# A third PSUM buffer for two kinds of products, and an earlier place for the tiles of one of them

## The chip, the core and the metric

The kernel runs on one core of a Trainium2 chip. The core has five engines that work side by side, each through its own list of instructions in order: TensorE (PE) for matrix products, VectorE (DVE), ScalarE (ACT), GpSimd (POOL) and SyncE (SP). Here POOL only issues indirect transfers and SP only plain ones. Products land in PSUM, which has eight banks of 128 partitions x 512 float32; everything else lies in SBUF. The metric is the device time of one execution in microseconds, the median of several runs.

## What is computed

One layer on 1024 frames of 1024 channels: a projection, two recurrent groups, an output projection, and then PEER, a retrieval over 16384 single-neuron experts. The change lies in PEER:

```python
q = (xb @ wq).reshape(TOK_BLOCK, PEER_HEADS, PEER_QDIM)
s1 = jnp.einsum('thd,kd->thk', q[..., :PEER_HALF], k1)
s2 = jnp.einsum('thd,kd->thk', q[..., PEER_HALF:], k2)
v1, i1 = lax.top_k(s1, PEER_TOPK); v2, i2 = lax.top_k(s2, PEER_TOPK)
...
sc, cidx = lax.top_k(cand, PEER_TOPK)
e = i1[cidx // PEER_TOPK] * PEER_NKEYS + i2[cidx % PEER_TOPK]
g = jax.nn.softmax(sc, axis=-1)
act = jax.nn.gelu(jnp.einsum('thkd,td->thk', u_tab[e], xb))
return jnp.einsum('thk,thkd->td', g * act, v_tab[e])
```

So each token picks 16 experts for each of 8 heads, weighs them by a softmax, and sums their output rows, each times the gelu of its input row with the token.

## The kernel before

The 1024 tokens are eight blocks of 128. Three blocks (NG) are **gathered**: the chosen rows of both tables are fetched, one token's expert to a partition, and worked on DVE, one row of 128x1024 at a time (`row`, summed into `hb`). Five blocks (ND = 5, TD = 640 tokens) are **dense**: for all 16384 experts, in 128 tiles of 128 experts, the kernel forms gelu(u x) and multiplies it with a weight that is zero where an expert was not chosen. Both run at once, since the first loads DVE and the transfers, and the second PE.

The program goes through these stages:

- **Up to 370 us**: projection, recurrent groups, output projection (`wop`). Then the norm's transposes (`x2t` of `xn`, split into `xDh` and `xDl`).
- **The query**: `qp`, PE products with weights `wqr` that SP loads and ACT and DVE split into `wqh` and `wql`, three products each for float32 accuracy. The result `qt` goes with `kT` into scores (`sp`, `sc`). The first head's query (`q_2940`, from weights `woh` and `wol` that lie in the output projection's pool) is made just ahead by `query0`. Scores of the dense blocks go to DRAM (`S_d`). DVE takes the top 16 of the gathered blocks meanwhile.
- **Build and ahead**: for each dense block, `topk` on DVE (`s` from `S_d`, `v`, `ix`, `scv`, `ci`, the softmax `ex` on ACT, `oh`, `if`), a PE transpose `gt` into `kt`, and then the dense weight matrix from one-hot products: for four tokens at a time DVE and ACT make `ohA` and `ohB` (DVE one of the four `ohB`, ACT the other three with six instructions), PE multiplies them (`gp`), ACT copies `gp` to `gs`, and SP stores `gs` to `G_d`, 2 MB at a time. Beside it `ahead` computes the first products of 97 of the 128 expert tiles: SP loads `ur`, ACT and DVE split it (`uh`, `ul`), PE makes two halves of 320 tokens in 24 matmuls each (`ap`, in `first`), ACT applies gelu (`aa`), and SP stores `aa` to `A_d`. `aa` lies in the pool `ph1`, three tiles of 128x640 float32.
- **Dense** (from 1512 us): the other 31 first products, and the second products `vp` and `total`, in an order written out by hand.

Three things set the order around the change. A planner (`Merge`) with estimated costs interleaves the threads as the code is recorded. The recording layer then orders the instructions of each engine again by its own estimate of when buffers come free, so another number of buffers moves instructions; only the dense stage is exempt. And a pool that is opened where another was closed makes its first users wait for the last users of the old one.

In PSUM, `ppa` has two banks (queries and first products), `ppt` two for `pt` and two for `pb` (the one-hot products), and two banks of the eight are used by no pool until the dense stage. In SBUF `ph1` is opened behind the query's pools `pq` and `pkg`, where these lay.

Of the kernel before, what the change touches and what calls it, by code (L numbers as in the profile page):

```python
# [7 lines left out]
F32 = mybir.dt.float32  # L8
# [7 lines left out]
PSUM = bass.MemoryType.PSUM  # L16
DRAM = bass.MemoryType.DRAM

P = 128
# [949 lines left out]
HALF = TD // 2  # L969
# [9 lines left out]
def peer(tc, a, cst, pools, h, nx, mg):  # L979
# [19 lines left out]
    ppa = pools.open("ppa", bufs=2, space=PSUM)  # L999
    ppt = pools.open("ppt", bufs=2, space=PSUM)  # L1000
    pa = lambda n: ppa.tile([P, 512], F32, tag="a", name=n)
    pt = lambda n: ppt.tile([P, 512], F32, tag="t", name=n)
    pb = lambda n: ppt.tile([P, 512], F32, tag="b", name=n)

    def split_to(hi, lo, src):
        S.activation(hi, src, AF.Copy)
# [319 lines left out]
    def load_split(pool, src, shape, tag):  # L1326
# [5 lines left out]
        split_to(h, lo, r)  # L1332
        return h, lo

    def first(dst, u):
        uh, ul = u
        for i in range(2):
            sl = slice(HALF * i, HALF * i + HALF)
            p_ = pa("ap")[:, :HALF]
            for k in range(8):  # L1340
                PE.matmul(p_, uh[:, k], xDl[:, k, sl], start=(k == 0), stop=False)
                PE.matmul(p_, ul[:, k], xDh[:, k, sl], start=False, stop=False)
                PE.matmul(p_, uh[:, k], xDh[:, k, sl], start=False, stop=(k == 7))
            yield
            S.activation(dst[:, sl], p_, AF.Gelu_apprx_tanh)
            yield
# [61 lines left out]
    def ahead():  # L1408
        fetch_u()
        yield  # L1410
        while made[0] < NA:
            kept = made[0] == NA - 1
            t = ph1.tile([P, TD], F32, name="aa", tag="hr", bufs=3)
            if kept:
                tile(0, 2).hr = t
            j = order[made[0]]
            for n, _ in enumerate(first(t, nextu[0])):
                if n == 0:
                    fetch_u(NA + 1)
                yield  # L1420
            if not kept:
                nc.sync.dma_start(A_d[j], t)
                mg.dma(320)
            made[0] += 1
            nextu.pop(0)
        mg.flag("ahead")
# [17 lines left out]
    mg.run([(1.0, topks()), gr], until="q")  # L1444
    mg.run([], until="chosen")
    pools.close("pkg", "pq")
    ph1 = pools.open("ph1")
    pk2 = pools.open("pk2", bufs=2)

    def build():  # L1450
# [13 lines left out]
        nc.sync.dma_start(gts[c], G_d[c])  # L1464

    mg.run([], until="g")
    pools.close("pk2", "ppt")


    ppr = pools.open("ppr", bufs=1, space=PSUM)  # L1470
# [18 lines left out]
    def second(p_, b, t, first, last, halves=(0, 1)):  # L1489
        bs = slice(b * P, b * P + P)  # L1490
        for i in halves:
            ns = slice(512 * i, 512 * i + 512)
            PE.matmul(p_[:, i], t.hh[:, bs], t.vl[:, ns], start=first, stop=False)
            PE.matmul(p_[:, i], t.hl[:, bs], t.vh[:, ns], start=False, stop=False)
            PE.matmul(p_[:, i], t.hh[:, bs], t.vh[:, ns], start=False, stop=last)
# [236 lines left out]
def body(tc, a):  # L1732
    nc = tc.nc
    pools = Pools(tc)
    pcst = pools.open("cst")
    ident = pcst.tile([P, P], F32, name="ident")
    make_identity(nc, ident)
    iota = pcst.tile([P, P], F32, name="iota")
    nc.gpsimd.iota(iota, pattern=[[1, P]], base=0, channel_multiplier=0, allow_small_or_imprecise_dtypes=True)
    mg = Merge(nc)  # L1740
    cst = dict(ident=ident, iota=iota)
    fpools, h, nx = front(tc, a, cst, ND, mg)
    peer(tc, a, cst, fpools, h, nx, mg)
    pools.close("cst")
# [65 lines left out]
```

## Time and profile before

| what | us |
|---|---|
| median of 3 runs | 2625.98 |
| lowest and highest run | 2618.97, 2636.02 |
| the profiled execution | 2620.74 |
| its span, first to last instruction | 2619.0 |

Over the whole span PE is busy 96%, PE's weight loads 87%, DVE 90%, ACT 50% and POOL 43% of the time, and the granted clock of PE is 0.985 on average. Busy shares are means over stages, and a busy PE is not PE at its peak. A row of instructions reads: start, duration, engine, line, operation, output<-inputs, and in brackets the idle time of the engine just before, with what ended it. A row of the waits reads: who waited for whom, the sum in us, how many times, the longest. A row of the chain reads: start, duration, what. The line is L146 nearly everywhere, since one helper records all instructions; so names of tiles tell the work apart.

### The profile page before, as it was taken

The page shows a single profiled execution, that of the slowest core. Times are in us where ns is not written, and L with a number is a line of the kernel's source. Part 1 is how long each engine was busy: PE and PEld are TensorE (multiplying, and loading weights), DVE is VectorE, ACT ScalarE, POOL GpSimd, SP SyncE. Part 2 cuts the span into 40 slices and gives each one's busy share as a digit, 9 for nine tenths or more (in the row PEclk, how much of TensorE's full clock was granted, in tenths as well). Part 3 has the DMA queues.
Part 4 walks back from the last instruction along what each step waited for, and adds up shares of the span by engine and source line. Part 5 has one row for each costly group of instructions (what it writes and reads, how often), then busy time and mean ns, then how long its engine had stood idle before and what let it go on. Part 6 is the DMA issues. An engine that isn't in the chain of part 4 may idle for free.

```text
span 2619.0 us, 40771 instructions
## 1 busy us (share of the span) xinstructions
PE 2503.9 (96%) x14623; PEld 2268.0 (87%) x14623; DVE 2365.3 (90%) x4556; ACT 1321.8 (50%) x2402; POOL 1130.8 (43%) x777
## 2 busy tenths in 40 slices
PE   7998999998999999999999999999999999999997
PEld 6776889998999999999999888888888888888885
DVE  7898659998999999999999399999989999999997
ACT  6566434332683965938739643333444433333442
POOL 0000000343664756848547054555445555554551
PEclk9999999999999999999999999999999999999999
DMA  5113124587899998999989899999989999999993
GB/s 183 30 43 108 61 91 137 189 287 285 305 394 310 360 388 307 397 344 349 399 297 377 277 336 343 346 343 342 342 321 346 344 342 341 343 347 341 340 339 132
DMA packets 302539, 753.31 MB, mean 288 GB/s; under 512 B 28928, under 2 KB 127424, under 8 KB 297600
## 3 DMA queue, kind: packets, MB, share of 16 engines
q0 software_dynamic: 110592, 402.70, 42.2%
q1 hardware_dynamic: 186048, 337.85, 36.4%
q10 hardware_dynamic: 5696, 10.15, 1.2%
q8 instruction: 115, 1.88, 0.3%
q14 instruction: 88, 0.72, 0.1%
HBM read 663.44 MB, written 85.98 MB: 286 GB/s over the span
## 4 chain that ended last, share of the span: by engine, by line
PE 62%; DVE 22%; DMA 7%; ACT 4%; issue 3%; ACTq 0%; SPq 0%; DVEq 0%
PE vp L146 26%; PE ap L146 17%; PE total L146 7%; PE qp L146 4%; DMA A_d<-aa 3%; PE gp L146 3%; PE wop L146 3%; DVE row L146 2%; DVE oh L146 2%; DVE ul L146 2%; DVE hb L146 2%; ACT ohB L146 1%; DVE ix L146 1%; DVE ci L146 1%; DVE v L146 1%
## 5 line engine op out<-in xcount | busy, mean ns | idle before, releaser
L1264 POOL DMA_INDIRECT row<-in_peer_u_dram,idx x384 | 564.8, 1471 | 958.5 <-DVE scv L146 471.0
L1264 POOL DMA_INDIRECT row<-in_peer_v_dram,idx x384 | 563.2, 1467 | 440.6 <-DVE hb L146 302.4
L146 PE MATMUL ap<-xDl,uh 128*128 128x320 f32 x2048 | 650.9, 318 | 14.3 <-ACT aa L146 12.0
L146 PE MATMUL ap<-xDh,ul 128*128 128x320 f32 x2048 | 642.8, 314 | 8.8 <-DVE ul L146 8.8
L146 PE MATMUL ap<-xDh,uh 128*128 128x320 f32 x2048 | 641.5, 313 | 0.0
L146 DVE SCALAR_TENSOR_TENSOR hb<-row,act,hb 128x1024 f32<-128x1024 f32 x384 | 491.5, 1280 | 4.6
L146 DVE CUSTOM_DVE_ANT_0 row<-row,xg 128x1024 f32<-128x1024 f32 x384 | 457.6, 1218 | 7.1 <-DMA row<-in_peer_u_dram,idx 6.6
L146 PE MATMUL vp<-vl,hh 128*128 128x512 f32 x1024 | 400.2, 391 | 9.4 <-DVE h L146 6.7
L146 PEld LDWEIGHTS ap<-xDl,uh 128*128 128x128 f32 x2048 | 390.4, 191 | 17.7 <-ACT aa L146 13.7
L146 PEld LDWEIGHTS ap<-xDh,ul 128*128 128x128 f32 x2048 | 390.5, 191 | 11.9 <-DVE ul L146 10.5
L146 PE MATMUL vp<-vh,hl 128*128 128x512 f32 x1024 | 400.2, 391 | 0.0
L146 PE MATMUL vp<-vh,hh 128*128 128x512 f32 x1024 | 399.0, 390 | 0.0
L146 PEld LDWEIGHTS ap<-xDh,uh 128*128 128x128 f32 x2048 | 389.8, 190 | 0.0
L146 ACT ACTIVATE gq<-gt 128x640 f32<-128x640 f32 x128 | 174.9, 1366 | 306.5 <-DVE hr L146 302.8
L146 PEld LDWEIGHTS vp<-vl,hh 128*128 128x128 f32 x1024 | 192.6, 188 | 50.4 <-DVE h L146 7.6
L146 PEld LDWEIGHTS vp<-vh,hh 128*128 128x128 f32 x1024 | 192.8, 188 | 40.9
L146 PEld LDWEIGHTS vp<-vh,hl 128*128 128x128 f32 x1024 | 192.5, 188 | 38.8
L146 ACT ACTIVATE ohB<-ohB,kt 128x128 f32<-128x128 f32 x480 | 205.3, 496 | 0.0
L146 ACT ACTIVATE aa<-ap 128x320 f32<-128x320 f32 x194 | 84.4, 436 | 237.2 <-PE ap L146 206.0
L146 PE MATMUL gp<-ohB,ohA 128*128 128x128 f32 x1280 | 183.7, 278 | 17.9 <-ACT gs L146 8.9
L146 DVE TENSOR_TENSOR h<-h,vp 128x1024 f32<-128x1024 f32 x128 | 155.7, 1217 | 48.8 <-PE vp L146 48.5
L146 PEld LDWEIGHTS gp<-ohB,ohA 128*128 128x128 f32 x1280 | 169.7, 192 | 22.2 <-ACT gs L146 9.7
(444 smaller groups left out, 4485.9 us busy)
## 6 DMA issues: line engine op xcount, KB each, us to landing
ur<-in_uT_dram SPq DMA_DIRECT2D x128, 512.0 KB, 6.6
vr<-in_peer_v_dram SPq DMA_DIRECT2D x128, 512.0 KB, 6.7
gt<-G_d SPq DMA_DIRECT2D x32, 1280.0 KB, 9.5
G_d<-gs SPq DMA_DIRECT2D x19, 2048.0 KB, 23.5
A_d<-aa SPq DMA_DIRECT2D x96, 320.0 KB, 7.5
hr<-A_d SPq DMA_DIRECT2D x96, 320.0 KB, 5.5
wqr<-in_wq_dram SPq DMA_DIRECT2D x31, 512.0 KB, 3.8
row<-in_peer_u_dram,idx POOLq DMA_INDIRECT x384, 7.4
```

The costliest lines, as they stand in the source:

```text
L146: return fn(*args, **kw)
L1264: G.indirect_dma_start(out=r, out_offset=None, in_=a["peer_v" if at >= P else "peer_u"], in_offset=bass.IndirectOffsetOnAxis(ap=idx[n][:, ...
```

## The change

`pb` gets a third buffer, and a new pool `ppx` of one bank takes every third `ap` as long as the build is not done (the flag `g`). Both together use the two idle banks; `ppx` is closed with `ppt`. `ph1` is opened ahead of `pq`, so its three tiles (7,680 bytes of each partition) lie below the query's pools instead of in their place, and `pq` and `pkg` lie 7,680 bytes higher.

```diff
     pt = lambda n: ppt.tile([P, 512], F32, tag="t", name=n)
-    pb = lambda n: ppt.tile([P, 512], F32, tag="b", name=n)
+    pb = lambda n: ppt.tile([P, 512], F32, tag="b", name=n, bufs=3)
+    ppx = pools.open("ppx", bufs=1, space=PSUM)
+    ph1 = pools.open("ph1")
...
+    turns = [0]
+
     def first(dst, u):
         uh, ul = u
         for i in range(2):
             sl = slice(HALF * i, HALF * i + HALF)
-            p_ = pa("ap")[:, :HALF]
+            turns[0] += 1
+            third = turns[0] % 3 == 0 and "g" not in mg.flags
+            p_ = (ppx if third else ppa).tile([P, 512], F32, tag="a", name="ap")[:, :HALF]
...
     pools.close("pkg", "pq")
-    ph1 = pools.open("ph1")
     pk2 = pools.open("pk2", bufs=2)
...
-    pools.close("pk2", "ppt")
+    pools.close("pk2", "ppx", "ppt")
```

The instructions are the same ones, in another order at some places. Three of them matter below.

**The start of the query, on SP.** The queue of SP before, with the semaphores that each waits for (each engine and each of eight transfer queues has one):

```order
L954 DMA X_d<-xn 128x1024 [waits DVE_49,PE_49]
L954 DMA X_d<-xn 128x1024 [waits DVE_49]
L954 DMA X_d<-xn 128x1024 [waits DMAHW2_49,DVE_49]
L1023 DMA wqr<-in_wq_dram 128x1024 [waits DMAHW4_49,PE_49]
L1023 DMA wqr<-in_wq_dram 128x1024 [waits DMAHW5_49]
```

And after the change:

```order
L954 DMA X_d<-xn 128x1024 [waits DVE_49,PE_49]
L954 DMA X_d<-xn 128x1024 [waits DVE_49]
L954 DMA X_d<-xn 128x1024 [waits DMAHW2_49,DVE_49]
L1025 DMA wqr<-in_wq_dram 128x1024 [waits DMAHW3_49,DMAHW4_49,PE_49,Activation_49]
L1025 DMA wqr<-in_wq_dram 128x1024 [waits DMAHW5_49]
```

The first load of query weights now waits for ACT too, and for another instruction of PE: before it was the last `wop` product, which reads `gh` and `gl`, and now it is the last product of `query0`. The pool `pq`, moved up, reaches 672 bytes into the place of the output projection's pool, whose last reader that product is.

**The start of the query, on PE.** The same place on PE, before:

```order
L146 MATMUL qp<-xGh,wol 128x384
L146 MATMUL qp<-xGh,woh 128x384
L146 MATMUL qp<-xGl,wqh 128x384
L146 MATMUL x2t<-ident,xn 128x128 x6
L146 MATMUL qp<-xGh,wql 128x384
```

And after:

```order
L146 MATMUL qp<-xGh,woh 128x384
L146 MATMUL x2t<-ident,xn 128x128 x8
L146 MATMUL sp<-kT,q_2940 128x128 x2
L146 MATMUL qp<-xGl,wqh 128x384
L146 MATMUL qp<-xGh,wql 128x384
```

The transposes and two score products of the first head now stand ahead of the first query product with loaded weights. The third score product of that head stays behind it.

**The build, on ACT.** ACT in the first block's one-hot products, before:

```order
L146 ACTIVATE gs<-gp 128x4x32x4
L146 ACTIVATE ohB<-iota,kt 128x128 x3
L146 ACTIVATE aa<-ap 128x320
L146 ACTIVATE ohB<-ohB,kt 128x128 x3
L146 ACTIVATE uh<-ur 128x1024
```

And after:

```order
L146 ACTIVATE gs<-gp 128x4x32x4
L146 ACTIVATE aa<-ap 128x320
L146 ACTIVATE ohB<-iota,kt 128x128 x3
L146 ACTIVATE ohB<-ohB,kt 128x128 x3
L146 ACTIVATE uh<-ur 128x1024
```

The eviction `aa` moved ahead of the one-hot rows `ohB` of the same group of tokens; so it did in some 20 groups of the 160. Near the end of the query, nine `ap` matmuls also stand between two `qp` matmuls of one accumulation now, where none stood, and in the fourth dense block one `aa` moved ahead of the softmax `ex`. The order of POOL is unchanged, and so is that of PE from the last `gp` on.

## The prediction

> **What bounds the kernel now.** I read the profile in this order: the chain that ended last, the busy time by stages, the waits of the one stage that the change aims at, and then single rows of the timeline. The stages first. The columns are the stretch and its length, the busy time of each engine with its number of instructions, PE's granted clock, the DMA share and GB/s.
>
> ```profile
> core 0: us, PE busy (x) PEld busy (x) DVE busy (x) ACT busy (x) POOL busy (x), PEclk, DMA share, GB/s
> 371.00:602.00 231.00, 221.20 (x1425) 213.78 (x1425) 218.87 (x809) 80.81 (x156) 62.76 (x46) 0.98 0.61 206
> 602.00:1372.00 770.00, 729.47 (x5073) 720.86 (x5071) 746.01 (x1919) 491.54 (x1176) 454.58 (x290) 0.98 0.95 344
> 1372.00:1511.60 139.60, 133.63 (x950) 132.41 (x950) 94.60 (x160) 114.76 (x276) 55.70 (x36) 0.99 0.92 325
> 1511.60:2619.00 1107.40, 1086.48 (x5283) 933.05 (x5281) 1018.95 (x1140) 437.77 (x487) 554.98 (x397) 0.99 0.90 329
> ```
>
> The rows are the query, build and ahead up to the fifth block's top-k, the rest of build and ahead, and the dense stage. In 602 to 1372 DVE has only 770.00 - 746.01 = 24.0 us free, PE 40.5, and the DMA engines are at 0.95. So PE's free time there is not all to be had: its one-hot products need what DVE makes. From 1372 on PE is the fuller engine, with 6.0 us free. The dense stage keeps its instructions and their order, so I hold it fixed.
>
> Now the waits from 602 to 1372, then PE's two from 1372 to 1511.6 that the change touches:
>
> ```profile
> ACT aa L146 <- DMA A_d<-aa: 30.8, 6, 8.6
> ...
> PE ap L146 <- ACT aa L146: 12.0, 6, 5.3
> DVE ohA L146 <- PE gp L146: 11.3, 5, 4.6
> ...
> PE gp L146 <- ACT gs L146: 7.3, 2, 3.8
> ...
> DVE ul L146 <- ACT uh L146: 4.5, 3, 2.2
> ...
> PE ap L146 <- ACT uh L146: 2.3, 1, 2.3
> PE gp L146 <- ACT gs L146: 1.6, 1, 1.6
> ```
>
> These are what more PSUM banks could buy: PE waits for an eviction `aa` of first products 12.0 us, for an eviction `gs` of one-hot products 7.3 and 1.6 us, together 20.9 us. ACT, which makes both evictions, itself stands 30.8 us until a store of `aa` has landed, for the three tiles of `ph1` are all taken.
>
> **Third bank for first products: 0.** The largest wait for `aa` is the first one, and here is where its time goes:
>
> ```profile
> 615.59 1.28 ACT L146 ACT_TABLE_LOAD   x1 [9.76 <-DMA S_d<-sc]
> 617.37 0.64 PE L146 MATMUL ap<-xDl,uh 128*128 128x320 f32 x1 [5.27 <-ACT aa L146]
> 619.07 0.49 DVE L146 MAX8 v<-s 128x8 f32<-128x128 f32 x2 [4.22 <-DMA s<-S_d]
> 678.04 0.33 PE L146 MATMUL gt<-ident,if 128*128 128x128 f32 x1 [1.99 <-DVE if L146]
> ```
>
> ACT waited for the scores' store, so two banks filled and PE stood 5.27 us. A third bank lets PE go on with 24 matmuls. But DVE's top-k of the first block, which starts at 619.07 on loaded scores, doesn't depend on that, and at 678.04 PE waits for that top-k (`if`) anyway. What PE gains at 617 it then waits longer at the transpose `gt`, since the numbers of `ap` matmuls ahead of each `gt` stay nearly the same in the new order. The other waits for `aa` are inside top-k stretches too. I take 0. Work that PE does earlier there would help only if it took work out of the stretch after 1372, and the new order takes none out that is worth a microsecond.
>
> **Third bank for one-hot products: 0.** The two waits for `gs`, with what ACT did just before:
>
> ```profile
> 765.63 0.44 ACT L146 ACTIVATE aa<-ap 128x320 f32<-128x320 f32 x1 [6.93 <-DMA A_d<-aa]
> 766.61 0.49 PE L146 MATMUL gp<-ohB,ohA 128*128 128x128 f32 x2 [3.56 <-ACT gs L146]
> 767.85 1.65 PE L146 MATMUL gp<-ohB,ohA 128*128 128x128 f32 x6 [0.76 <-ACT ohB L146]
> 769.54 0.69 DVE L146 TENSOR_TENSOR ohA<-iota,kt 128x512 f32<-128x512 f32 x1 [4.62 <-PE gp L146]
> ...
> 1253.21 0.44 ACT L146 ACTIVATE aa<-ap 128x320 f32<-128x320 f32 x1 [7.97 <-DMA A_d<-aa]
> 1254.18 0.49 PE L146 MATMUL gp<-ohB,ohA 128*128 128x128 f32 x2 [3.78 <-ACT gs L146]
> ```
>
> At both places ACT stood 6.93 and 7.97 us at an `aa` whose tile was still being stored. The `gs` behind it on ACT was late for that reason, not for want of a PSUM bank alone. With a third bank PE may start the next group two matmuls (0.49 us) sooner, but the other rows of that group, `ohB`, lie on ACT behind the same `aa`: at 767.85 PE waits for them at once. So the store decides, and the change makes neither the stores faster nor the tiles of `aa` more. DVE's 4.62 us at 769.54 hang on the same thing. I take 0.
>
> [...]
>
> **`aa` ahead of `ohB` on ACT: 0, at worst +16.** In some 20 groups ACT now meets `aa` before the six `ohB` of the same tokens. Where `aa` needn't wait, that moves them by one `aa`, 0.44 us, within what PE and DVE have queued. Where it does wait, they are late by its whole wait. The price of one set from the page's groups:
>
> ```profile
> L146 ACT ACTIVATE ohB<-ohB,kt 128x128 f32<-128x128 f32 x480 | 205.3, 496 | 0.0
> ```
>
> The other three of a set are of the same shape, so six cost at most 6 x 0.496 = 3.0 us. Six waits of `aa` (the 30.8 us), each with a full set now behind it instead of hidden in it, give at most 6 x 3.0 = 17.9, of which the two at 765 and 1253 already have such rows behind them (0.76 us there), so some 16. With three tiles in `ph1` as before, the same six waits should recur at about the same places, and 20 of 160 groups is one in eight; I expect less than one hit, and take 0. Nine `ap` matmuls that now stand inside the query fall in a hole that PE has there:
>
> ```profile
> 544.45 0.41 PE L146 MATMUL qp<-xDh,wql 128*128 128x320 f32 x1 [1.76 <-DVE wql L146]
> ```
>
> Nine matmuls at 3.52/24 = 0.147 us (the row of 1042.28 below) are 1.3 us, inside the 1.76. If that hole is gone, they cost at most 1.3 us, and save as much later.
>
> **`ph1` moved ahead: +3.** The tiles of `ph1` cost nothing themselves. But the query's pool now reaches into the place of the output projection's, so the first load of `wqr` waits for `query0`'s last product, which reads `woh`:
>
> ```profile
> 370.83 3.98 DMA wqr<-in_wq_dram
> ...
> 374.63 0.34 PE L146 MATMUL qp<-xGh,woh 128*128 128x384 f32 x1
> 374.83 1.06 ACT L146 ACTIVATE wqh<-wqr 128x1024 fp32r<-128x1024 f32 x1 [1.55 <-DMA wqr<-in_wq_dram]
> 375.92 1.22 DVE L146 TENSOR_TENSOR wql<-wqr,wqh 128x1024 fp32r<-128x1024 f32 x1 [0.29 <-ACT wqh L146]
> 376.32 0.45 PE L146 MATMUL qp<-xGl,wqh 128*128 128x384 f32 x1 [1.35 <-ACT q L146]
> 377.20 0.44 PE L146 MATMUL qp<-xGh,wql 128*128 128x384 f32 x1
> ...
> 383.51 1.22 DVE L146 TENSOR_TENSOR wql<-wqr,wqh 128x1024 fp32r<-128x1024 f32 x1
> 384.64 0.48 DVE L146 MAX8 vg<-sc 128x8 f32<-128x128 f32 x2
> ```
>
> The load leaves at 374.63 + 0.34 = 374.97 instead of 370.83, 4.1 us later. It lands at 374.97 + 3.98 = 378.95; `wqh` takes 1.06, so the first product with loaded weights can start at 380.0 instead of 376.3 (+3.7), and `wql` ends at 381.2 instead of 377.1. That frees a weight buffer for the third load: 3.98 + 1.06 + 1.22 later, at 387.5, its `wql` is through. On DVE the first MAX8 of the gathered blocks' top-k stands right behind that `wql`, in both orders. It starts at 384.64 now, so it comes 2.9 us later. Behind SP's first load the other `wqr` loads are queued, and all move with it. PE covers part of the hole with transposes that now stand earlier, and both engines are nearly full in the query (DVE 231.00 - 218.87 = 12.1 us free, PE 9.8), so I let the 2.9 stay, rounded to +3. The ends are 0, if the free 12.1 us take it up, and +4.1, the whole delay. `kT` waits likewise, behind `q` on ACT, but is needed only by score products, which stand behind the query's on PE's list.
>
> **The sum.** 0 + 0 + 0 + 3 = +3 on the profiled execution's 2620.74 us, that is 2623.7. The median of the runs is 2625.98, 5.2 above that execution, so the forecast for a median is 2626 + 3 = 2629.
>
> **Rivals.** A: the banks pay fully. Then the 20.9 us go. Beside them, PE's clock falls after its longest stalls:
>
> ```profile
> 617.00:621.00 4.00, 3.63 (x16) 3.63 (x17) 1.93 (x14) 1.59 (x3) 0.94 (x1) 0.59 1.02 411
> ...
> 769.50 5.54 PE ap L146 x24
> 1042.28 3.52 PE ap L146 x24
> ```
>
> After the stall at 617 the granted clock is 0.59, and the 24 `ap` matmuls that follow the stall at 766 take 5.54 us instead of 3.52, a loss of 2.0. The three long stalls shown (5.27, 3.56 and 3.78 us) would give 6 us more at 2.0 each. [...] 20.9 + 6 - 3 = 24 us faster, about 2602; past 1% only if the shorter stalls lose by the clock as well. Against it: DVE has just 24.0 us free in 602 to 1372, and the stores stay. For the bound of my range I take from DVE's side what hangs on PE and ACT there, 11.3 + 4.5, and PE's 1.6 + 2.3 after 1372: 19.7 us, so 2606.
>
> B, slower: `aa` ahead of `ohB` at the places where ACT waits for a store. It gives up to +16 beside the +3, 2645, if nearly all of the six waits fall on moved groups. It decides from the second hit on. To get past 1% it would have to come with waits of `aa` about twice as long as the 30.8 us. For it speaks that DMA is at 0.95 busy; against it that ACT is only busy 491.54 of 770.
>
> C: the delay in the query is taken up by DVE's free 12.1 us, and nothing else changes: 2626. The change does then not do anything to the time, though its waits on PSUM are gone.
>
> **How the numbers follow.** My forecast has 0.60, A 0.10, B 0.15, C 0.15. The time is that of the forecast, 2629. The range goes from A's bounded end 2606 to 2644, just under B's end; it leaves out A's full gain and B's tail, under 2 in 10. A measurement of this kernel can tell about 1% (26 us) from no change: faster by more than that needs A in full with the clock's part at the shorter stalls, 0.07 of its 0.10; slower needs more than all of B, 0.06; within it 0.87.
>
> **What would show it.** The delay is right if the first `wqr` load leaves near 375 and the first MAX8 starts near 387.5. The zero for first products is right if PE's wait for `aa` at 617 shrinks and its wait for `if` or for `st` at the next `gt` grows as much. The zero for one-hot products is right if ACT's wait for the store of `aa` stays near 30.8 us and PE's wait for `gs` turns to one for `ohB`. B shows as PE and DVE waiting for ACT's `ohB` behind such a wait. The forecast is wrong if DVE's busy time in 602 to 1372 fills the stretch, that is if that stretch gets shorter by 10 us or more, or if those waits for stores grow.

## The result: slower by 0.57%, inside the range

| | before | after |
|---|---|---|
| median, us (20 runs each) | 2624.04 | 2640.46 |
| lowest to highest | 2617.14 to 2636.02 | 2627.43 to 2646.64 |
| the profiled execution, its span | 2620.74, 2619.0 | 2645.85, 2644.0 |

The ratio is 1.0057, with a 95% interval of 1.0044 to 1.0070: 0.0057 x 2624 = 15 us slower, between 11.5 and 18.4. The forecast was +3. The profiled execution is 5 us above the median of its kernel and that of before 3 us below, so the rows, 25 us apart, show more than the mean loss.

The busy time by stages in the changed kernel, in the columns and at the times of the first table of the prediction:

```profile
371.00:602.00 231.00, 218.61 (x1411) 210.03 (x1410) 213.41 (x801) 80.71 (x155) 58.43 (x42) 0.99 0.59 195
602.00:1372.00 770.00, 719.66 (x5003) 713.37 (x5002) 733.92 (x1899) 488.18 (x1169) 441.71 (x287) 0.96 0.94 340
1372.00:1511.60 139.60, 133.96 (x946) 132.69 (x945) 100.39 (x172) 105.94 (x267) 63.67 (x43) 0.98 0.92 322
```

In the same 770 us both full engines did less: DVE 733.92 us against 746.01, PE 719.66 against 729.47, and PE's granted clock fell from 0.98 to 0.96. So the time went into more waiting, not more work. The waits of that stage:

```profile
ACT aa L146 <- DMA A_d<-aa: 18.9, 4, 8.1
PE gp L146 <- DVE ohB L146: 18.7, 7, 10.7
PE ap L146 <- DVE ul L146: 17.0, 6, 10.4
...
DVE ohA L146 <- PE gp L146: 13.6, 7, 5.3
DVE ul L146 <- ACT uh L146: 13.3, 3, 10.9
...
ACT uh L146 <- DMA ur<-in_uT_dram: 11.0, 1, 11.0
...
PE gp L146 <- ACT ohB L146: 8.3, 2, 5.0
```

And three of the same rows before:

```profile
PE ap L146 <- DVE ul L146: 7.8, 6, 2.8
...
PE gp L146 <- DVE ohB L146: 2.9, 2, 2.7
...
ACT uh L146 <- DMA ur<-in_uT_dram: 0.6, 1, 0.6
```

The waits that the third banks were made for are gone: neither PE's wait for `aa` (12.0 us before) nor the one for `gs` (7.3) stands in the list. In their place PE waits for `ul` (17.0, before 7.8) and for `ohB` of DVE (18.7, before 2.9). And ACT, which stood less for stores of `aa` (18.9, before 30.8), stands 11.0 us for a load of `ur`, where it stood 0.6 before. Not each of these sums tells something: the profiles of e1 and e7 below, which have the order of before in the build, show 16.8 and 8.8 us for `ul` and 37.0 and 21.9 for the stores of `aa`. The sum for `ohB` of DVE (7.8 and 3.9 there) and the single wait of 11 us for `ur` stand out.

The place of that load is the second dense block. Here are SP's queue, ACT, DVE and PE there, in the changed kernel:

```profile
914.66 0.37 SPq L1221 DMA_DIRECT2D G_d<-gs  x1
920.91 18.59 SPq L1428 DMA_DIRECT2D A_d<-aa  x1
939.59 1.47 SPq L1330 DMA_DIRECT2D ur<-in_uT_dram  x2
...
953.54 1.06 ACT L146 ACTIVATE uh<-ur 128x1024 fp32r<-128x1024 f32 x1 [11.05 <-DMA ur<-in_uT_dram]
954.63 1.23 DVE L146 TENSOR_TENSOR ul<-ur,uh 128x1024 fp32r<-128x1024 f32 x1 [10.86 <-ACT uh L146]
...
956.86 2.05 PE L146 MATMUL gp<-ohB,ohA 128*128 128x128 f32 x8 [10.69 <-DVE ohB L146]
```

Behind the 2 MB store of `G_d`, the next issue on SP stands 18.59 us, and the two loads of `ur` go only when it is through, 25 us after the store was issued. ACT waits for one of them with the copies `gs` and the rows `ohB` of the following tokens queued behind it, DVE waits for ACT, and PE for both. Before, the same store let the queue go after 17.5 us, and neither ACT nor PE stopped for it (the 0.6 us above are all that ACT waits for `ur` in that stage):

```profile
903.88 0.37 SPq L1219 DMA_DIRECT2D G_d<-gs  x1
905.45 15.94 SPq L1328 DMA_DIRECT2D ur<-in_uT_dram  x1
921.49 0.41 SPq L1422 DMA_DIRECT2D A_d<-aa  x1
```

How much this costs is read from the transposes `gt` that begin the second and the third block's one-hot products. Before:

```profile
849.03 0.27 PE L146 MATMUL gt<-ident,gd 128*128 128x128 f32 x1
...
1017.60 0.27 PE L146 MATMUL gt<-ident,gd 128*128 128x128 f32 x1
```

And after:

```profile
855.31 0.27 PE L146 MATMUL gt<-ident,gd 128*128 128x128 f32 x1
...
1037.92 0.27 PE L146 MATMUL gt<-ident,gd 128*128 128x128 f32 x1
```

The block took 168.6 us before and 182.6 after: 14 us of the 25 that lie between the two profiled executions. The rest is spread: 2.4 us up to the last `wop`, 3.0 from there to the first `gt`, small amounts in the other blocks (the fourth is 4.3 us shorter), and some 4 in the dense stage, whose instructions and order are the same. So some of the 25 is chance.

The other part is the start of the query, as forecast, but not in the size. In the changed kernel the stretches around its first product with loaded weights, and the rows that lead to the first MAX8:

```profile
382.50:388.50 6.00, 5.43 (x17) 4.97 (x17) 2.44 (x2) 1.06 (x2) 0.00 (x0) 0.50 0.56 161
388.50:392.00 3.50, 3.50 (x22) 3.23 (x20) 0.23 (x1) 1.70 (x4) 0.00 (x0) 0.98 0.06 23
```

```profile
377.48 7.86 SPq L1025 DMA_DIRECT2D wqr<-in_wq_dram  x4
...
381.57 1.14 PE L146 MATMUL sp<-kT,q 128*128 128x128 f32 x4 [2.30 <-DVE xDl L146]
...
390.30 0.49 ACT L146 ACTIVATE qt<-qp 128x384 f32<-128x384 f32 x1 [6.58 <-PE qp L146]
390.69 1.05 ACT L146 ACTIVATE wqh<-wqr 128x1024 fp32r<-128x1024 f32 x1
391.77 1.23 DVE L146 TENSOR_TENSOR wql<-wqr,wqh 128x1024 fp32r<-128x1024 f32 x1 [6.79 <-ACT wqh L146]
392.91 0.48 DVE L146 MAX8 vg<-sc 128x8 f32<-128x128 f32 x2
```

The first weight load leaves at 377.48, after `query0`'s last product, as forecast (the last `wop` ends 2.4 us later in this execution). But PE had stood just before (2.30 us in the second row), its granted clock is 0.50 from 382.5 to 388.5, and the product lasts until 390.3. ACT waits 6.58 us for it with the third `wqh` behind it, and DVE 6.79 us for that.

### The profile page after: what moved, and what is told of

The parts are those of the page before. It is cut to its first block, busy times and chain, and to the rows that moved or that the text cites. A ratio compares the mean times of both kernels' runs of the same rounds, so it can differ in the third digit from the quotient of the medians.

```text
span 2644.0 us, 40780 instructions
## 1 busy us (share of the span) xinstructions
PE 2510.7 (95%) x14623; PEld 2275.3 (86%) x14623; DVE 2365.8 (89%) x4556; ACT 1322.8 (50%) x2402; POOL 1121.8 (42%) x777
## 3 DMA queue, kind: packets, MB, share of 16 engines
q0 software_dynamic: 110592, 402.70, 41.8%
q1 hardware_dynamic: 186048, 337.85, 36.2%
## 4 chain that ended last, share of the span: by engine, by line
PE 58%; DVE 23%; DMA 8%; issue 6%; ACT 3%; POOL 1%; ACTq 0%; SPq 0%; DVEq 0%; POOLq 0%
PE vp L146 26%; PE ap L146 15%; PE total L146 6%; DMA A_d<-aa 4%; PE wop L146 3%; PE gp L146 3%; PE qp L146 2%; DVE row L146 2%; DVE hb L146 2%; DVE ul L146 2%; DVE oh L146 2%; DVE ix L146 1%; ACT ohB L146 1%; POOL row L1266 1%; DVE v L146 1%
## 5 line engine op out<-in xcount | busy, mean ns | idle before, releaser
L1266 POOL DMA_INDIRECT row<-in_peer_v_dram,idx x384 | 554.6, 1444 | 455.3 <-DVE hb L146 311.0
L146 PE MATMUL ap<-xDh,ul 128*128 128x320 f32 x2048 | 646.4, 316 | 17.8 <-DVE ul L146 17.7
L146 DVE CUSTOM_DVE_ANT_0 row<-row,xg 128x1024 f32<-128x1024 f32 x384 | 457.7, 1217 | 12.7 <-DMA row<-in_peer_u_dram,idx 12.3
L146 PE MATMUL gp<-ohB,ohA 128*128 128x128 f32 x1280 | 193.8, 281 | 29.7 <-DVE ohB L146 18.7
L146 PEld LDWEIGHTS gp<-ohB,ohA 128*128 128x128 f32 x1280 | 178.1, 195 | 33.5 <-issue 15.0
```

The lines of the kernel that those rows point to most:

```text
L146: return fn(*args, **kw)
L1266: G.indirect_dma_start(out=r, out_offset=None, in_=a["peer_v" if at >= P else "peer_u"], in_offset=bass.IndirectOffsetOnAxis(ap=idx[n][:, ...
```

## The experiments

The theory at first: two separate costs, the query's start and an order in the build, each to be had alone. Ratios are to runs of the kernel before on the same chip, 23 to 35 of them.

### e1 to e4: the change in its parts

e1 keeps only the new place of `ph1`:

```diff
     pb = lambda n: ppt.tile([P, 512], F32, tag="b", name=n)
+    ph1 = pools.open("ph1")
...
-    ph1 = pools.open("ph1")
```

> Only the new place of ph1, all PSUM pools as before. Theory 1 (two separate costs): the query starts about 4 us late and ends 3 to 4 us late, and nothing else changes, since the order of every engine is that of the kernel before from the query on: +3 to +4 us, ratio 1.001 to 1.0015. Rival (the late query shifts everything behind it into worse places): the whole +15 us, ratio 1.0057.

Measured: 1.0020 (1.0004 to 1.0035), +5 us. All orders behind the query's first 20 us or so are those of before, so this is the query's delay alone; it isn't the whole loss.

e2 keeps both third buffers, with `ph1` at its old place; e3 only the bank `ppx` for `ap`; e4 only the third buffer of `pb`.

> Both third PSUM buffers, ph1 at its old place. Theory 1: the query is that of before, and the build loses 11 to 12 us, ratio 1.0042 to 1.0047, with a stall of PE of about 10 us in the second dense block where ACT waits for ur. Rival (all is the query's delay): 1.000. Rival (the banks help by themselves): below 0.998.

Measured: 1.0041 (1.0025 to 1.0057), +11 us. Parts e1 and e2 together give 0.61%, against 0.57% for the change: within the intervals they add up.

> Only the third bank for first products. The order on DVE, ACT and SP is that of the change. Theory 1: the loss is that of the order, so it is as e2, ratio 1.004 to 1.005. Rival (the third one-hot bank makes the loss): 1.000.

Measured: 1.0026 (1.0007 to 1.0044).

> Only the third bank for one-hot products; SP's order is that of the kernel before, ACT's nearly so. Theory 1: no change, ratio 0.999 to 1.001, PE's waits for gs become waits for ohB. Rival (one-hot products are held by their banks): PE's and DVE's waits at gp fall by 7 to 19 us and the time by 0.3% or more.

Measured: 1.0003 (0.9987 to 1.0018). In its profile PE's wait for `gs` between 602 and 1372 is gone and the one for `ohB` is larger:

```profile
PE ap L146 <- ACT aa L146: 11.7, 6, 5.6
PE gp L146 <- ACT ohB L146: 9.4, 4, 7.0
PE gp L146 <- DVE ohB L146: 8.1, 5, 3.7
```

So the third one-hot bank alone does nothing to the time that these runs can tell, though it moves some 340 instructions on DVE too, and the build's loss comes with the third bank for first products. Whether both banks together cost more than that one alone is not settled by the intervals. In the second block's one-hot products PE stopped in both e2 (the first row) and e3:

```profile
940.03 2.05 PE L146 MATMUL gp<-ohB,ohA 128*128 128x128 f32 x8 [4.16 <-DVE ohB L146]
```

```profile
942.85 2.05 PE L146 MATMUL gp<-ohB,ohA 128*128 128x128 f32 x8 [6.42 <-ACT ohB L146]
```

In the changed kernel it stopped 10.69 us there, and in none of before, e1 and e4.

### e5, e6 and e9: is it SP's order?

With the third `ap` bank two loads of `ur`, the 20th and the 36th, stand behind a store of `aa` that they stood ahead of. The second of them is the load above. (Three more pairs of neighbours change places: the 24th and the 31st load of `ur` with loads of `s` and `xg`, and the 63rd store of `aa` with a load of `nf`. They were not tried apart.) e5 does the two to the kernel before, by edges that only set the order of issue:

```diff
+    stores, SWAP = {}, {19: 15, 35: 31}
...
+            if m in SWAP:
+                with tc.issue_after(stores[SWAP[m]]):
+                    nextu.append(load_split(pu, a["uT"][order[m]], [8, P], "u"))
```

> The kernel before, with two rows of SP's queue exchanged and nothing else: the 20th and the 36th load of ur each stand behind the store of aa (the 16th and the 32nd) that they stood ahead of, as they do with the third bank for first products. Theory (the loss in the build is SP's order: the store can't go until its aa is made, then stands behind the 2 MB store, and the load is late behind both): +5 to +8 us, ratio 1.002 to 1.003, and PE stops for 4 to 10 us in the second block's one-hot products. Rival (the loss is from ACT's order, aa ahead of ohB): 1.000, no such stop.

Measured: 1.0005 (0.9984 to 1.0026), and no stop of over 2 us in that place.

e6 uses the third `ap` bank from the 34th tile on, so that SP's order stays that of before:

```diff
-            third = turns[0] % 3 == 0 and "g" not in mg.flags
+            third = turns[0] % 3 == 0 and turns[0] > 66 and "g" not in mg.flags
```

> Both third PSUM buffers at ph1's old place, but the third bank for first products is used from the 34th tile on only. SP's order is then that of the kernel before. Theory (SP's order): 0.999 to 1.001, like the third one-hot bank alone, and no stop of over 4 us in the second block. Rival (a third bank for first products costs wherever it is used): about half of the loss of e3 and more, 1.0013 or above.

Measured: 1.0022 (1.0003 to 1.0041). No stop in that place, as the theory says, but not without loss either.

e9 puts the two rows back in e2, with nothing else changed:

```diff
+            if m in SWAP:
+                tc.add_manual_dep(stores[SWAP[m]], lastu[0].name, ...)
```

> As e2 (both third PSUM buffers, ph1 at its old place), with the two rows of SP's queue put back: the 20th and the 36th load of ur again ahead of the store of aa. Nothing else differs from e2 on any engine. Theory (those two rows cost where PE and ACT run ahead as they do with the third bank): the stop of PE in the second block's one-hot products (4 to 11 us in e2, e3 and the changed kernel) is gone, and the ratio falls from 1.0041 to 1.000 to 1.002. Rival (the order of PE and ACT costs by itself, as e5 and e6 suggest): 1.003 to 1.005, and the stop stays or another takes its place.

Measured: 1.0028 (1.0004 to 1.0052). In its profile the stop is still there, though the load now stands first behind the store:

```profile
912.02 0.37 SPq L1220 DMA_DIRECT2D G_d<-gs  x1
915.28 21.03 SPq L1331 DMA_DIRECT2D ur<-in_uT_dram  x1
...
946.80 1.06 ACT L146 ACTIVATE uh<-ur 128x1024 fp32r<-128x1024 f32 x1 [6.94 <-DMA ur<-in_uT_dram]
...
950.12 2.05 PE L146 MATMUL gp<-ohB,ohA 128*128 128x128 f32 x8 [6.58 <-DVE ohB L146]
```

The theory of SP's order falls: those two rows make no loss alone that these runs can tell, and putting them back doesn't take the stop away. What is the same in e2, e3, e9 and the changed kernel is that the queue stands longer behind this store: 24.3 us from issue to release in e9 (915.28 + 21.03 - 912.02), 24.8 in the changed kernel, 21.8 in e2 and 24.4 in e3, against 17.5 before and 16.3 to 17.8 in e1, e4, e5 and e6.

### e7 and e10: room for the query's pool

e7 is e1 with one buffer fewer for `sc`, so that the query's pool ends below the output projection's place:

```diff
-                    sc = pq.tile([P, 256], F32, tag="sc", name="sc", bufs=6)
+                    sc = pq.tile([P, 256], F32, tag="sc", name="sc", bufs=5)
```

> ph1 at its new place as in e1, but with five instead of six buffers for sc, so that the query's pool no longer reaches into the place of the output projection's. The order of all engines is that of the kernel before. Theory (the loss of e1 is the wait of the first weight load for the last product of query0): 1.000, and the first MAX8 is back at its old distance from the output projection's end. Rival (the loss comes from the place itself, or from the fall of e1's figure by chance): 1.002 as e1.

Measured: 0.9998 (0.9977 to 1.0019). The first `wqr` load leaves at 375.40 in its trace, right behind the last `wop` (374.98 + 0.39), and the first MAX8 follows 14.1 us behind that `wop`, as before (384.64 - 370.80 = 13.8); in the changed kernel it is 19.7 and in e1 19.5 us. In the two traces:

```profile
375.40 14.51 SPq L1024 DMA_DIRECT2D wqr<-in_wq_dram  x5
...
389.47 0.48 DVE L146 MAX8 vg<-sc 128x8 f32<-128x128 f32 x2
```

```profile
376.19 15.70 SPq L1024 DMA_DIRECT2D wqr<-in_wq_dram  x5
...
391.45 0.48 DVE L146 MAX8 vg<-sc 128x8 f32<-128x128 f32 x2
```

The first pair is e7, the second e1, whose last `wop` ended at 371.55 + 0.39 = 371.9. So e1's delay comes from the overlapped place. That the time came back with it fits, but the intervals of e1 and e7 overlap, so it isn't shown by them. Nor does the delay always last: from the last `wop` to the first `gt` of the build, e1 takes 5.8 us longer than before, the changed kernel 3.0 and e7 1.0.

e10 is the changed kernel with e7's and e9's repairs.

> The changed kernel with both repairs: five buffers for sc, so that the query starts as before, and the two rows of SP's queue put back. Theory of two separate costs: 1.000 to 1.002, 10 us or more faster than the changed kernel. Rival (ACT's and PE's order in the build costs by itself): 1.003 to 1.005, as e2.

Measured: 1.0051 (1.0028 to 1.0073). The first MAX8 is back (13.9 us behind the last `wop`), but not the time, as is to be expected after e9: the build's part isn't repaired. The 0.2% of the query is too small to be told in this interval.

### e8: the 2 MB stores on another queue

```diff
-                    nc.sync.dma_start(G_d[js, :, t0:t0 + GT]...
+                    nc.scalar.dma_start(G_d[js, :, t0:t0 + GT]...
```

> The kernel before, with the 2 MB stores of G_d issued on ACT's queue instead of SP's. Theory (SP's loads and stores stand behind them in one queue): SP's issues no longer stand for 10 to 20 us, ACT's 30.8 us of waits for stores of aa shrink by half or more, and the time falls by 5 to 20 us, ratio 0.992 to 0.998. Rival (the DMA engines are full at a share of 0.95, so that whatever is moved only waits elsewhere): 0.999 to 1.001.

Measured: 1.0304 (1.0278 to 1.0331), 80 us slower. SP's queue then doesn't stand (the issue behind the first of these stores takes 0.33 us), and ACT's waits for stores of `aa` from 602 to 1372 are 0, as the theory says. But some 900 instructions each on ACT and DVE moved with it, and in that stretch PE was busy only 674.16 us, with 29.8 us of waits for `ul` and 25.2 for `ohB` of DVE. So it tells nothing on the queue by itself; it shows that taking those waits away doesn't help when the order changes so much.

### e11 and e12: DVE's gather rows

Comparing where things stand in DVE's order with and without the third `ap` bank shows one large move, in the second dense block. The gelu of the first gathered block's `act` stands on ACT behind 37 copies `gs` instead of 32 (the expectation below counts one less). The rows `hb`, which need it, follow on DVE: at the 40th `ohA` 128 of the gathers' row instructions are done instead of 135, and the seven are caught up to three by the 64th, at the time of the store above. Some 40 of the third block's top-k instructions fill their place (by the 40th `ohA` 643 MAX8, FIND_INDEX8 and MATCH_REPLACE8 are done instead of 604). In e4 and e6 the gather rows and the top-k stand there as before. e11 does this to the kernel before, by edges that tie each of the block's 32 `ohA` to its neighbouring rows:

```diff
+    TAB = [127, 127, 128, 128, 128, 128, 128, 128, 130, 132, ...
...
+                    tc.add_manual_dep(frm(), to().name, mybir.DependencyInfo(
+                        mybir.DependencyClass.NoSync, mybir.DependencyReason.DATA), reason="order")
```

> The kernel before, with DVE's gather rows of the second dense block put where the third bank for first products puts them: the gelu of the first gathered block's act stands behind 36 copies gs instead of 31, and up to seven rows that stood ahead of the 40th ohA stand behind it and are caught up by the 64th. Nothing else of weight moves. Theory (the rows, and with them their transfers, bunch at the second 2 MB store of that block): SP's queue stands about 24 us behind that store instead of 17 to 18, ACT waits for ur 5 us or more, PE stops 4 us or more in that block, and the time is +5 to +8 us, ratio 1.002 to 1.003. Rival (the loss is spread over ACT's moved aa and PE's order): 1.000, and the store's time stays 16 to 20 us.

Measured: 1.0021 (1.0007 to 1.0034), +5 us. The edges moved more than the gather rows: the 40 top-k instructions came forward as in e3, and one load of `ur` on SP went ahead of the load of `xg`, as there. So e11 tests this whole move and not the seven rows alone. Its trace, in SP's queue and where ACT and PE stop:

```profile
930.55 0.37 SPq L1237 DMA_DIRECT2D G_d<-gs  x1
932.72 25.55 SPq L1440 DMA_DIRECT2D A_d<-aa  x1
...
969.95 0.44 ACT L146 ACTIVATE aa<-ap 128x320 f32<-128x320 f32 x1 [14.02 <-DMA A_d<-aa]
...
970.44 0.64 PE L146 MATMUL ap<-xDl,uh 128*128 128x320 f32 x1 [7.97 <-ACT aa L146]
```

```profile
848.53 0.27 PE L146 MATMUL gt<-ident,gd 128*128 128x128 f32 x1
...
1027.74 0.27 PE L146 MATMUL gt<-ident,gd 128*128 128x128 f32 x1
```

The second block takes 179.2 us, 10.6 more than before, and the loss is that of e3 within the intervals. This execution was the slowest of e11's twelve, 12.7 us above their median, so its rows show more than the mean loss. The size was as expected and the place nearly so: the store that holds the queue is the third of the block (27.7 us from issue to release; 22.3 before) rather than the second (22.4; 17.5 before), and what waits behind it is a store of `aa`, for which ACT stands 14.02 us, more than a load of `ur`.

e12 is the undoing: e2, with the rows of that block tied to the places that they have before.

> As e2 (both third PSUM buffers, ph1 at its old place), with DVE's gather rows of the second dense block pinned to the places of the kernel before. Theory: the second 2 MB store of that block lets SP's queue go after 16 to 20 us, PE's stop in that block is under 4 us, and the ratio falls from 1.0041 to 1.000 to 1.002. Rival: 1.003 to 1.005.

Measured: 1.0039 (1.0025 to 1.0053). The second store's hold is down to 19.0 us (916.47 + 18.05 - 915.52) and the stop at 936 is gone:

```profile
915.52 0.37 SPq L1238 DMA_DIRECT2D G_d<-gs  x1
916.47 18.05 SPq L1347 DMA_DIRECT2D ur<-in_uT_dram  x1
```

But the time didn't come back. The tie holds the one-hot rows of the block's start behind the gather rows, whose gelu ACT still makes late (behind 35 `gs`), the top-k still stands early, and in this profile the first eight groups of the block's `ohA` take 32 us instead of 20. So e12 put a new wait in the old one's place and doesn't tell how much the rows are worth inside the change.

How the rows may reach SP's queue is read from the amounts that the queues moved in the 17 us from that store on. The columns are packets, MB, and their share of the 16 DMA engines' time; q0 carries the gathered rows (402.70 MB in the whole profile of before, which holds 768 loads of 512 KB) and q1 SP's plain transfers (337.85 MB). Before:

```profile
q0 software_dynamic: 1161, 4.23, 61.0%
q1 hardware_dynamic: 3421, 2.53, 44.5%
```

And in the changed kernel:

```profile
q0 software_dynamic: 1377, 5.03, 72.5%
q1 hardware_dynamic: 1728, 1.91, 31.1%
```

The DMA engines were full in those 17 us (a share of 1.06 before and 1.04 in the changed kernel), and the gathers took more of them while the store went out, 72.5% against 61.0%. They moved 5.0 to 5.1 MB in e2, e3, e9 and e10 as well, where the queue stood 21.8 to 24.4 us; 4.7 MB in e11 (22.4 us), 4.4 in e12 (19.0), and 4.2 to 4.6 in e1, e4, e5, e6 and e7 (16.3 to 20.4). So the longer hold goes with the gathers' larger part, and both moved in e11 and e12, where edges move the rows.

## Why the prediction was right in its range and wrong in its size

- **What bounds the kernel**: right. Both engines are nearly full from 602 to 1372 (PE 719.66 and DVE 733.92 of 770 us in the changed kernel), and taking away PE's waits on PSUM (12.0 and 7.3 us) gave no time.
- **Third bank for one-hot products, 0**: right. e4 is 1.0003, and PE's wait turned from `gs` to `ohB`, as worked out. The sign that ACT's wait for stores stays near 30.8 us did not hold (18.3 in e4), but this sum varies as much between profiles of one order.
- **Third bank for first products, 0**: this is the step that failed. The prediction costed it by PE's place alone ("What PE gains at 617 it then waits longer at the transpose"). That held in kind only: the wait for `aa` at 617 went, but what grew was a wait for `ul`, 10.41 us a tile later, and not the wait at the next transpose, which was 1.99 us and is gone. The time is what it had wrong: e3 is +0.26%, and with the other third buffer +0.41%, some 7 to 11 us of the 15. The working counted the rows of `ap` on PE and the `aa` and `ohB` on ACT; it passed over one gelu on ACT that moved by five groups, and with it seven gather rows on DVE, with their transfers of 512 KB, and some 40 top-k instructions. e11 shows that this move alone costs about 5 us (2 to 9) in the kernel before.
- **`aa` ahead of `ohB`, and rival B**: the sign of B, but not its place. ACT's waits for stores of `aa` did not grow (30.8 and 18.9 us). The queueing behind a waiting ACT that B describes is what the profile shows, with the load of `ur` as the thing waited for (11.05 us on ACT, 10.69 us on PE behind it), which stood in SP's queue behind the 2 MB store.
- **`ph1` moved, +3**: the mechanism was right: the load left when the forecast said, +5 us in e1 (1 to 9, so +3 isn't excluded), 0 in e7 with the overlap taken away. The delay at the first MAX8 was forecast too small, since two terms were missed. The third `wqh` stands on ACT behind `qt`, which waits for a whole product (6.58 us), and that product ran at a granted clock of 0.50 from 382.5 to 388.5, after PE's stop of 2.30 us. The first MAX8 came 5.9 us later by its distance to the last `wop` (19.7 - 13.8), not 2.9. Rival A read the fall of the clock off longer stalls (0.59 after 5.27 us). PE's gaps here are 0.81 and 2.30 us with the short transposes between, each shorter than the three stalls shown there, and the trace doesn't settle what set the clock down.
- **The sum**: +3 forecast, +15 measured; 5 of it from the query and 11 from the build. That the range held is luck in part: its upper end was drawn from ACT's waits for stores of `aa` with work queued behind them, and neither the move on DVE nor the full delay of the query, some 5 us each in the runs, was in it.

What stays open is the build's share in detail. e11 shows that the move on DVE is enough for some 5 us, but not whether the gather rows or the top-k instructions make them. Six profiles with an early third `ap` bank (the changed kernel, e2, e3, e9, e10, e12) have 175 to 183 us for the second block, where the others have 169 to 171, without e8 (182.9) and e11. A longer second block isn't yet a longer kernel: in e3's profile it is 10.1 us longer, but the first and the fourth are 4.3 and 6.3 us shorter. That the gathers slow the 2 MB store rests on the amounts above and on e11 and e12; that this wait makes the loss in time isn't shown, since e12 did not bring the time back. Whether the rest is ACT's moved `aa`, which e6 may hint at with +0.22%, wasn't settled. No version was found that beats the kernel before.

## What to carry to other kernels

Where a scheduler places the instructions, another buffer can be a change of order on several engines, not only a bank: look in the new order for single instructions that have moved far and have many others behind them, on the engines that the buffer doesn't touch too. Before a pool is moved, see whose place its end reaches, as 672 bytes here delayed a whole stage's first load (in e1 it left at 376.19, 4.3 us behind the last `wop`, and in e7, without the overlap, right behind it). And where large stores and small urgent loads share one queue, look at how long a store holds it, and at the work that feeds the other transfers meanwhile: here the queue stood 24.8 us behind one 2 MB store, ACT stood 11.05 us for a load behind it and PE 10.69 us for ACT and DVE.

## What was not expected of the hardware

- In the profile of before, the issue on SP's queue next behind a 2 MB store stood itself, while the store's own issue took 0.37 to 0.86 us: 18 of 19 such issues took 8.8 to 22.0 us, and one 3.1. What comes behind it on the queue stood too: in the changed kernel the two loads of `ur` above left 24.9 us after the store was issued.
- With the same order on all engines, the hold behind the same store was 17.5 us in the profile of before and 20.4 in that of e7, so a few us of any single profile here are chance.
- In the profiles of e9 and e10, ACT stood 17.80 and 21.5 us at the end of the query with no releaser on the core that the profile names. Others show nothing of that size there:

```profile
612.65 0.44 ACT L146 ACTIVATE qt<-qp 128x320 f32<-128x320 f32 x1 [17.80 <-remote]
```

What it was isn't known. From the first MAX8 to the first `gt` these two take 302.9 and 305.1 us, and the others, without e8, 291 to 295, so the reading of e9 above goes by the second block and not by its span.
